# Spreading the running maxima of an mLSTM over the partitions: transpositions into PSUM in place of GpSimd's partition broadcast

## The chip, the cores and the metric

One core of one Trainium2 chip runs the whole program. The metric is the device time of one execution in microseconds, the median of three runs. Times inside an execution come from one profiled execution and are counted from the start of its span.

## The reference, cut to what matters

The program is one layer of an encoder for 512 tokens of 1024 columns, all in float32. Three token mixers work side by side on one input projection: multi-scale pooling, a bidirectional mLSTM with 4 heads of 64, and attention with 8 query heads. Their outputs are concatenated and projected. Then come cross attention into 256 memory tokens and a routed mixture of 16 experts, whose weights (24 MB for each expert) are read from HBM once.

The change touches the mLSTM alone. For one head and one direction, with the running sums b of the forget gates' logarithms and the input gates' logarithms i, it computes (chunks of tokens, `m_st` the running maximum):

```
dmat = where(lower, bcum[j] - bcum[s] + li[s], -inf)
m_j  = maximum(bcum[j] + m_st, max_s dmat[j, s])
a    = exp(dmat - m_j) * (q_j . k_s)
h_j  = sum_s a[j, s] v_s / maximum(|sum_s a[j, s]|, exp(-m_j))
```

With a_s = i_s - b_s and M_j the running maximum of a_s over s up to j (at least 0), the weight of s for j is exp(a_s - M_j), and m_j = b_j + M_j. The backward direction is the same from the last token on.

## The kernel before

Tokens lie on the partitions in four tiles of 128 (`NT`), or along the free dimension, 512 columns, where a row is wanted. Products that need precision are made of a high and a low part, three matmuls in `mm3` (L124 to L127); `split` (L129) makes the parts, a cast on ScalarE (L132) and a subtraction on VectorE or GpSimd (L133).

SBUF is divided into arenas whose words the program hands out and takes back by hand (`Arena`, `Buf`, `Ring`). PSUM has four pools: `mm` with three banks, `tr` and `sc` with two each, and `oo` with one. Tiles of a pool are handed out in the order of the program, so whoever asks for `oo` waits until its last owner has been read.

Two streams of work are emitted in turn by `weave`: a chain and a filler, cut into pieces with an assumed TensorE time. A planner then orders the instructions of each engine by its own estimate of time; every engine works off its list strictly in order. The queue of SP issues all transfers, also in order.

The stages around the change, in order:

- Attention in two halves (L449 to L466): scores, maximum, exponential, scaling by the reciprocal sum (L424 on GpSimd for odd token tiles, L426 on VectorE for even ones), transposition of the weights (L434), product with the values into `oo` (L444). The second half is woven with the mLSTM's projections, in the midst of which `gates()` runs.
- `gates()` (L527): from the gates, per token and for 8 columns (4 heads of each direction), the sums b (`bc`), a (`ag`) and, by a transposition of `az` (L560) and a scan along the free dimension (L562, L564), the running maxima as rows: `Mrow[d]` holds in partition 32 h the row of head h. Four transpositions for each direction (L568) bring them back to tokens on partitions, and L569 adds `bc` to them to make m; L571 makes exp(-m).
- The mLSTM (`mlstm()`, L642) as chain, woven with `fill_kv()` (L731) as filler: the pooling projection, the pooling mixer (`pool_mix()`, L709; sums on GpSimd L714 to L718, VectorE L720 to L722, TensorE L725 into `oo`), and keys and values of the memory. For each head and direction `decay(h, d)` (L621) makes the weights exp(a_s - M_j): the row of M is spread over all partitions, four exponentials on ScalarE (L628) take it with a as bias, and GpSimd masks the diagonal block (`affine_select`, L631). `decay` is called one head ahead. Then come the scores of the head (L650, by `mm3`, into `sc`), their product with the weights on VectorE (L655), the product with the values (L667, into `tr`), the division (L674 to L684) and the norm of the head (L688 to L692). `out_turn` (L635) transposes two heads' outputs through `oo` (L638).
- The output projection: `w_out` is loaded in eight pieces through a ring of three staging buffers (L788), cast and split; `x` is loaded (L807) into words that the mLSTM's buffers had; `out_proj` (L815) adds the product to `x` (L825).
- Cross attention, the choice of tokens, and the experts. Expert weights come in pieces of 1 MB into slots; a slot is opened when the words under it are free, and each load is issued from SP's queue (`issue`, L858; L866, L874).

Of the kernel before, what the change touches and what calls it, by code (L numbers as in the profile page):

```python
# [12 lines left out]
AF = mybir.ActivationFunctionType  # L13
# [16 lines left out]
class Arena:  # L30
    """A stretch of SBUF, one tile, whose words are handed out and taken back by hand."""
# [26 lines left out]
class Buf:  # L58
    """f: its words as float32, r: as float32r. Of several arenas, it lies in the first with room."""
# [39 lines left out]
def build(nc, tc, A, out, ne=NE, dbg=None):  # L99
# [29 lines left out]
    def split(src, h, l, scale=None, le=None):  # L129
        """h + l = src * scale, h of 12 bits."""  # L130
        if scale is None:
            C.copy(h.bitcast(F32R), src)  # L132
            (le or V).tensor_tensor(l.bitcast(F32R), src, h, op=ALU.subtract)  # L133
        else:
            C.activation(h.bitcast(F32R), src, AF.Identity, scale=scale)
            V.scalar_tensor_tensor(l.bitcast(F32R), src, scale, h, op0=ALU.mult, op1=ALU.subtract)
# [19 lines left out]
    # Two streams of work are emitted in turn: generators yield the time on TensorE of each piece.  # L156
# [14 lines left out]
    # ------------------------------------------------------------ constants, small inputs  # L171
# [42 lines left out]
    def load_w(i, parts=2):  # L214
        """Chunk i of the weights, as high and low parts."""
        if i >= len(plan):
            return
        name, src, c0, n = plan[i]
        hb, lb = wring.next(), wring.next()
        st = KT // parts  # L220
        for j in range(parts):
            a, b = j * st, (j + 1) * st
            rbuf = raw.next()
            SP.dma_start(rbuf.f[:, 0:st, :n], src[:, a:b, c0:c0 + n])
            split(rbuf.f[:, 0:st, :n], hb.f[:, a:b, :n], lb.f[:, a:b, :n], le=(G if j % 2 and i < 7 else V))
        W[name] = (hb, lb, n)
# [6 lines left out]
    # ------------------------------------------------------------ x transposed, with the gain, split  # L233
    SP.dma_start(cols.f, A["cols"])
    # the tables of ScalarE and the full clock of TensorE, ahead of the data
# [29 lines left out]
    # ------------------------------------------------------------ tables of the rotation  # L265
# [35 lines left out]
    # ------------------------------------------------------------ products with the chunks  # L301
# [23 lines left out]
    def head_norms(q1, nh):  # L325
        """1 / rms of the nh heads, by token tile."""
# [9 lines left out]
    def rope(t, q1, nh, which, y, variants):  # L336
        """Head norm and rotation of nh heads of a token tile, as [hi, lo] of each."""
# [15 lines left out]
    def turn(t, dest):  # L353
        """[hi; lo] of the heads of a token tile, transposed."""
        p = TR()
        for h in range(4):
            T.transpose(p[:, h * 128:(h + 1) * 128], qsb.f[:, t, h * 128:(h + 1) * 128], idn)
        for h, d in enumerate(dest):
            (C.copy if h % 2 else V.tensor_copy)(d.r[:, t * 128:(t + 1) * 128], p[:, h * 128:(h + 1) * 128])

    # keys and values, then the queries of heads 0 to 3
# [34 lines left out]
    # row of rstd over tokens, on all partitions  # L396
# [9 lines left out]
    # ------------------------------------------------------------ attention  # L406
# [61 lines left out]
    # ------------------------------------------------------------ mLSTM projections, conv  # L468
# [55 lines left out]
    # ------------------------------------------------------------ gates of the mLSTM  # L524
    gs = Mrow = None

    def gates():  # L527
# [3 lines left out]
        nf, ef, lf, bc, ag, mt, em, of = (gs.f[:, i] for i in range(8))  # L531
        V.tensor_scalar(nf, fpre, -1.0, None, op0=ALU.mult)
# [4 lines left out]
        # running sums of log f over tokens, both ways  # L537
# [27 lines left out]
        for d in range(2):  # L565
            p = OO()
            for t in range(NT):
                T.transpose(p[:, t * 128:(t + 1) * 128], Mrow[d].f[:, t * 128:(t + 1) * 128], idn)  # L568
            V.tensor_tensor(mt[:, :, 4 * d:4 * d + 4], p.rearrange("p (t h z) -> p t h z", t=4, z=32)[:, :, :, 0],  # L569
                            bc[:, :, 4 * d:4 * d + 4], op=ALU.add)  # L570
        C.activation(em, mt, AF.Exp, scale=-1.0)  # L571
        az.free()
# [30 lines left out]
    # ------------------------------------------------------------ mLSTM  # L603
    ag, em = gs.f[:, 4], gs.f[:, 6]
    Mb = Ring(f0, 2, [S])
# [5 lines left out]
    # segments of the weights of a direction: tile st covers tokens js  # L611
# [9 lines left out]
    def decay(h, d):  # L621
        """exp(a_s - M_j), s on partitions."""
        c = 4 * d + h
        mb, w = Mb.next(), Wr.next()
        G.partition_broadcast(mb.f, Mrow[d].f[32 * h:32 * h + 1, :])
        for st in range(NT):
            o, js = seg[d][st]
            C.activation(w.f[:, o:o + js.stop - js.start], mb.f[:, js], AF.Exp, scale=-1.0, bias=ag[:, st, c:c + 1])  # L628
# [13 lines left out]
    def mlstm():  # L642
        nxt = [decay(0, 0), decay(0, 1)]
        for h in range(4):
# [40 lines left out]
            # norm of the head, output gate  # L685
# [9 lines left out]
    # ------------------------------------------------------------ pooling mixer, memory keys and values  # L695
# [81 lines left out]
    # ------------------------------------------------------------ output projection  # L777
# [6 lines left out]
    def load_pair(src, k, c0, hb, lb, le=None, scale=None):  # L784
        """Rows of k and k + 1, 512 columns."""
# [14 lines left out]
    for b in (raw, Mb, Wr, hsum, htmp, mst, nst, gs, gt, og, *mv, rows, rrow, ones, tri, *Mrow):  # L800
        b.free()
# [31 lines left out]
    # ------------------------------------------------------------ cross attention  # L833
# [5 lines left out]
    where = {}  # the slot of each chunk under way  # L839
    once = {}  # the slots that serve once, as their words have another use later  # L840
# [3 lines left out]
    # columns of the down projection of the last expert, in parts that end ever sooner  # L844
    LAST = (512, 256, 256)

    def down_part(e, j):
        """The blocks of rows and the columns in chunk j."""
# [9 lines left out]
    def issue(s):  # L858
# [8 lines left out]
        else:  # L867
# [3 lines left out]
            # in halves where TensorE waits for the first one  # L871
# [19 lines left out]
    # router weights, with the gain of the norm  # L891
# [44 lines left out]
    def warm(ap, n):  # L936
        """Keeps TensorE at its full clock while it has to wait; the product is not used."""
# [3 lines left out]
    def top_k(i, j):  # L941
        """The 64 largest of candidates i, in order, to the front of candidates j."""
# [120 lines left out]
    # squares go to words that are written again before they are read  # L1063
# [62 lines left out]
    # ------------------------------------------------------------ ring of expert weights  # L1126
# [13 lines left out]
    # ------------------------------------------------------------ choice of tokens  # L1140
    # the 64 largest of two lists in falling order: the larger of each and its counterpart of the other, reversed
# [3 lines left out]
    # above the threshold, then equal to it, each in the order of the tokens  # L1145
# [20 lines left out]
    def gather(gi, step=4):  # L1166
        """Tokens of two experts, transposed, normed."""
# [29 lines left out]
    # the sum over the experts, in the slots that serve once; x stays as it is until the last gather is done  # L1197
    acc = [s.f.rearrange("p (t d) -> p t d", d=D) for s in once["acc"]]

    def scatter(e, ts, c0, w):  # L1200
        """The columns c0 to c0 + w of the tiles ts, side by side in one bank."""
# [34 lines left out]
    for e in range(ne):  # L1236
# [33 lines left out]
        if e == ne - 1:  # L1270
            # the table of the square root, ahead of its use
# [16 lines left out]
    # ------------------------------------------------------------ the last expert's end, and the final norm  # L1288
# [3 lines left out]
    # the gain of the final norm, along the columns in all partitions  # L1292
# [53 lines left out]
def layout(inp):  # L1346
    """Host side: the small inputs packed, and constants of the shapes."""
# [57 lines left out]
```

## Time and profile before

| what | value |
|---|---|
| median of three runs | 1378.24 us (1375.71, 1378.44, 1378.24) |
| span of the profiled execution, first to last instruction | 1375.2 us; no time of its own is listed beside the three |
| TensorE busy | 1234.7 us, 90% of the span |
| VectorE, ScalarE, GpSimd busy | 443.2, 274.1 and 123.4 us |
| mean granted TensorE clock | 0.965 of full speed |
| read from HBM | 431.74 MB, 315 GB/s over the span |
| chain that ended last | TensorE 61%, DMA 23%, VectorE 7%, issue 4%, ScalarE 3%, GpSimd 1% |

Busy time says how long an engine had an instruction in work; matmuls are pipelined, so their lengths overlap. A full granted clock of 1.00 is 2.4 GHz, 0.50 is 1.2 GHz. Idle time in square brackets stands before an instruction on its own engine, with the instruction that released it; "issue" is time in which the engine waited for nothing that the profile shows. In the rows PE is TensorE, PEld its weight load, DVE VectorE, ACT ScalarE, POOL GpSimd and SP the engine whose queue issues the transfers.

### The profile page before, as it was taken

Reading aid. Unit: us, or ns where it says so; the run is one execution under the profiler, and the core shown is the slowest. Engines: PE = TensorE matmul, PEld = TensorE weight load, DVE = VectorE, ACT = ScalarE, POOL = GpSimd, SP = SyncE. Lnnn points to the kernel's source line nnn. Section 1 sums busy time; section 2 is a strip of 40 time slices with the busy share of each in tenths; the row PEclk is TensorE's granted clock in tenths of the full one; section 3 lists DMA queues with packets and bytes.
Section 4 is the critical chain, followed back from the end, with each engine's and each line's share of the span. In section 5 each row is a group of like instructions: output and inputs, shape, how many; then the busy total and the mean of one; then the engine's idle time right before and its main releaser. Section 6 shows DMA issues by size and latency. Waiting matters only on the chain.

```text
span 1375.2 us, 15752 instructions
## 1 busy us (share of the span) xinstructions
PE 1234.7 (90%) x6225; PEld 632.4 (46%) x6225; DVE 443.2 (32%) x1034; ACT 274.1 (20%) x579; POOL 123.4 (9%) x165
## 2 busy tenths in 40 slices
PE   9999763779998999999999999989988998998886
PEld 8976553668885334334343324323322432332223
DVE  5997731653564011221221221202112120202213
ACT  6565531322441100101001010000101000010113
POOL 5433122220200000000000000000000000000002
PEclk9999975879999999999999999999999999999998
DMA  8321120032587999999999999999999999999996
GB/s 278 90 65 47 52 91 0 31 107 62 213 337 274 367 417 416 419 416 419 414 421 414 420 415 417 418 415 421 414 420 415 417 418 414 420 414 421 415 412 213
DMA packets 97338, 434.87 MB, mean 316 GB/s; under 512 B 7536, under 2 KB 25584, under 8 KB 64496
## 3 DMA queue, kind: packets, MB, share of 16 engines
q1 hardware_dynamic: 97264, 433.87, 78.9%
q8 instruction: 49, 0.80, 0.2%
q14 instruction: 25, 0.20, 0.0%
HBM read 431.74 MB, written 2.10 MB: 315 GB/s over the span
## 4 chain that ended last, share of the span: by engine, by line
PE 61%; DMA 23%; DVE 7%; issue 4%; ACT 3%; POOL 1%; SPq 0%; DVEq 0%; ACTq 0%; POOLq 0%
PE mm L1249 19%; PE sc L1280 8%; PE oo L1249 6%; PE tr L1178 5%; DMA r_f<-in_expert_w_down 4%; PE mm L125 3%; PE mm L127 3%; PE mm L126 3%; DMA rq_f<-in_expert_w_down 3%; DMA ra_f<-in_expert_w_down 3%; DMA rb_f<-in_expert_w_gu 3%; DMA rq_f<-in_expert_w_gu 3%; DMA r2a_f<-in_expert_w_gu 3%; PE tr L1206 2%; PE tr L1207 2%
## 5 line engine op out<-in xcount | busy, mean ns | idle before, releaser
L1216 DVE SCALAR_TENSOR_TENSOR f_f<-tr,f_f 128x512 f32<-128x512 f32 x112 | 79.9, 746 | 91.5 <-PE tr L1207 91.5
L1249 PE MATMUL mm<-rq_f,rg_f 128*64 128x512 f32 x388 | 97.3, 604 | 6.6 <-DMA rq_f<-in_expert_w_gu 6.6
L133 DVE TENSOR_TENSOR rp_r<-sc,rp_r 128x512 fp32r<-128x512 f32 (+1 forms) x31 | 21.1, 682 | 216.1 <-ACT rp_r L132 216.1
L1249 PE MATMUL mm<-r_f,rg_f 128*64 128x512 f32 x324 | 80.3, 602 | 5.8 <-DMA r_f<-in_expert_w_gu 5.4
L1299 POOL TENSOR_SCALAR f_f<-f_f 128x128 f32<-128x128 f32 x8 | 3.3, 433 | 907.5 <-PE tr L1194 880.4
L1178 PEld LDWEIGHTS tr<-f_f 128*128 128x128 f32 x512 | 61.7, 191 | 45.6 <-issue 23.5
L1178 PE MATMUL tr<-f_f 128*128 128x128 f32 x512 | 70.8, 284 | 7.5 <-ACT rg_f L1185 4.7
L1262 DVE TENSOR_TENSOR fb_f<-mm,fb_f 128x512 f32<-128x512 f32 x16 | 11.1, 692 | 204.9 <-PE mm L1249 199.0
L1261 ACT ACTIVATE fb_f<-mm 128x512 f32<-128x512 f32 x32 | 19.0, 597 | 278.6 <-PE mm L1249 278.6
L1280 PE MATMUL sc<-rq_f,fb_f 128*64 128x512 f32 x280 | 64.7, 599 | 3.7 <-DMA rq_f<-in_expert_w_down 3.6
L1185 ACT ACTIVATE rg_f<-tr,f_f 128x128 f32<-128x128 f32 x32 | 11.8, 368 | 271.7 <-PE tr L1178 181.6
L1249 PE MATMUL mm<-rb_f,rg_f 128*64 128x512 f32 x240 | 59.6, 603 | 3.8 <-DMA rb_f<-in_expert_w_gu 3.8
L1183 DVE TENSOR_SCALAR rg_f<-tr,f_f 128x128 f32<-128x128 f32 x32 | 11.2, 351 | 157.7 <-PE oo L1249 78.7
L1280 PE MATMUL sc<-r_f,fb_f 128*64 128x512 f32 x240 | 57.3, 600 | 4.5 <-DMA r_f<-in_expert_w_down 4.5
L1206 PE MATMUL tr<-rp_r 128*128 128x512 f32 (+1 forms) x132 | 58.1, 444 | 3.3 <-ACT rp_r L132 1.4
L132 ACT CAST rp_r<-sc 128x512 fp32r<-128x512 f32 (+1 forms) x31 | 17.9, 579 | 200.1 <-PE sc L1280 200.1
L1207 PE MATMUL tr<-rp_r 128*128 128x512 f32 (+1 forms) x132 | 53.2, 407 | 1.8 <-DVE rp_r L133 1.1
L1206 PEld LDWEIGHTS tr<-rp_r 128*128 128x128 f32 x132 | 24.5, 187 | 55.8 <-DVE f_f L1216 31.5
L1249 PEld LDWEIGHTS mm<-rq_f,rg_f 128*64 128x64 f32 x388 | 24.3, 136 | 55.5 <-issue 34.6
L1249 PE MATMUL mm<-r2a_f,rg_f 128*64 128x512 f32 x192 | 46.5, 603 | 3.4 <-DMA r2a_f<-in_expert_w_gu 3.4
L127 PE MATMUL mm<-r_r,rb_r 128*128 128x256 f32 (+2 forms) x160 | 46.7, 296 | 0.0
L1249 PE MATMUL oo<-rq_f,rg_f 128*64 128x512 f32 x172 | 45.1, 593 | 0.0
(452 smaller groups left out, 2225.0 us busy)
## 6 DMA issues: line engine op xcount, KB each, us to landing
rq_f<-in_expert_w_gu SPq DMA_DIRECT2D x70, 1024.0 KB, 19.8
r_f<-in_expert_w_gu SPq DMA_DIRECT2D x54, 1024.0 KB, 19.8
rb_f<-in_expert_w_gu SPq DMA_DIRECT2D x45, 1024.0 KB, 19.8
rq_f<-in_expert_w_down SPq DMA_DIRECT2D x35, 1024.0 KB, 20.0
r2a_f<-in_expert_w_gu SPq DMA_DIRECT2D x32, 1024.0 KB, 19.8
r_f<-in_expert_w_down SPq DMA_DIRECT2D x30, 1024.0 KB, 20.0
ra_f<-in_expert_w_gu SPq DMA_DIRECT2D x26, 1024.0 KB, 19.9
rb_f<-in_expert_w_down SPq DMA_DIRECT2D x18, 1024.0 KB, 18.9
```

The costliest lines, as they stand in the source:

```text
L125: T.matmul(o, lh, rh, start=start, stop=False)
L126: T.matmul(o, lh, rl, start=False, stop=False)
L127: T.matmul(o, ll, rh, start=False, stop=stop)
L132: C.copy(h.bitcast(F32R), src)
L133: (le or V).tensor_tensor(l.bitcast(F32R), src, h, op=ALU.subtract)
L1178: i = T.matmul(o, x.f[:, t, kt * 128:(kt + 1) * 128], flat(g.f[:, t]), start=(t == 0), stop=(t == NT - 1))
L1206: T.matmul(pp[:, i * w:(i + 1) * w], GT.r[:, ts_], flat(yh.r)[:, cs], start=True, stop=False)
L1207: T.matmul(pp[:, i * w:(i + 1) * w], GT.r[:, ts_], flat(yl.r)[:, cs], start=False, stop=True)
L1216: V.scalar_tensor_tensor(ao, p, g, ao, op0=ALU.mult, op1=ALU.add)
L1249: T.matmul(pg[2 * half + b][64 * ab:64 * ab + 64], xs.f[:, k, el * 64:(el + 1) * 64], wv[:, :, ab], start=(k == 0), stop=(k == KT - 1))
L1261: C.activation(hsl.f[:, b], pg[b], AF.Silu)
L1280: T.matmul(py[c][64 * ab:64 * ab + 64], hT.f[:, blk, 64 * ab:64 * ab + 64], wv[:, ab, c * 512:(c + 1) * 512], start=(blk == 0), stop=(blk ...
```

## The change

`gates()` keeps the running maxima by token, before the addition of `bc`, in `mk_`, the words of `nf`, whose content is no longer needed there. `decay()` spreads a column of it: for each token tile the column is read as a 128x128 block (the same column 128 times) and transposed into a quarter of an `oo` bank, so that every partition holds the row M_j. ScalarE's exponentials read that bank. The ring `Mb` of two rows in SBUF is gone, and the rows `Mrow` are given back at the end of `gates()`.

```diff
@@ gates()
         nf, ef, lf, bc, ag, mt, em, of = (gs.f[:, i] for i in range(8))
+        mk_ = nf
 ...
             p = OO()
             for t in range(NT):
                 T.transpose(p[:, t * 128:(t + 1) * 128], Mrow[d].f[:, t * 128:(t + 1) * 128], idn)
-            V.tensor_tensor(mt[:, :, 4 * d:4 * d + 4], p.rearrange("p (t h z) -> p t h z", t=4, z=32)[:, :, :, 0],
-                            bc[:, :, 4 * d:4 * d + 4], op=ALU.add)
+            V.tensor_copy(mk_[:, :, 4 * d:4 * d + 4], p.rearrange("p (t h z) -> p t h z", t=4, z=32)[:, :, :, 0])
+        V.tensor_tensor(mt, mk_, bc, op=ALU.add)
         C.activation(em, mt, AF.Exp, scale=-1.0)
-        az.free()
+        for b in (az, *Mrow):
+            b.free()
@@ ahead of the mLSTM
-    Mb = Ring(f0, 2, [S])
@@ decay(h, d)
         c = 4 * d + h
-        mb, w = Mb.next(), Wr.next()
-        G.partition_broadcast(mb.f, Mrow[d].f[32 * h:32 * h + 1, :])
+        mb, w = OO(), Wr.next()
+        for t in range(NT):
+            T.transpose(mb[:, t * 128:(t + 1) * 128], gs.f[:, 0, t, c:c + 1].to_broadcast([128, 128]), idn)
         for st in range(NT):
             o, js = seg[d][st]
-            C.activation(w.f[:, o:o + js.stop - js.start], mb.f[:, js], AF.Exp, scale=-1.0, bias=ag[:, st, c:c + 1])
+            C.activation(w.f[:, o:o + js.stop - js.start], mb[:, js], AF.Exp, scale=-1.0, bias=ag[:, st, c:c + 1])
@@ after the mLSTM
-    for b in (raw, Mb, Wr, hsum, htmp, mst, nst, gs, gt, og, *mv, rows, rrow, ones, tri, *Mrow):
+    for b in (raw, Wr, hsum, htmp, mst, nst, gs, gt, og, *mv, rows, rrow, ones, tri):
```

With `Mb` and `Mrow` gone, buffers that are handed out later lie elsewhere. In the arena `f0`, `Wr` moves from word 3208 to 2696 and the norm statistics `nst` from 1544 to 1032; `x` later takes words 376 to 4472, 1024 for each token tile. In `rq`, the pooling input `up` moves from word 7020, the words of `az`, to 5988, where `Mrow` (5996 to 7020) was. Comments are left out of the changed file as well.

## Rows read from the trace of the kernel before

**Rows 1.** The profile's page, its parts 1 and 2: busy time, share of the span and instructions of each engine; then the span in 40 equal slices of 34.4 us, in tenths.

```profile
PE 1234.7 (90%) x6225; PEld 632.4 (46%) x6225; DVE 443.2 (32%) x1034; ACT 274.1 (20%) x579; POOL 123.4 (9%) x165
...
PE   9999763779998999999999999989988998998886
...
PEclk9999975879999999999999999999999999999998
DMA  8321120032587999999999999999999999999996
```

**Rows 2.** Busy time by stretches: the stretch (us), its length, then for each engine the busy us and in brackets the number of instructions, the granted TensorE clock as a share of full speed, the DMA share and GB/s. First pieces of the stretch, then the whole stretch and its neighbours.

```profile
174.20:180.30 6.10, 6.06 (x29) 6.06 (x30) 2.04 (x7) 2.91 (x4) 2.09 (x2) 0.50 0.06 16
207.30:211.10 3.80, 3.75 (x11) 3.18 (x12) 0.38 (x1) 3.80 (x10) 0.79 (x1) 0.51 0.00 0
232.50:239.10 6.60, 6.60 (x24) 5.63 (x24) 1.17 (x2) 0.00 (x0) 0.71 (x2) 0.50 0.00 0
248.70:251.90 3.20, 3.19 (x9) 2.16 (x10) 3.03 (x12) 0.69 (x1) 0.60 (x3) 0.50 0.48 159
251.90:273.50 21.60, 21.60 (x150) 19.60 (x149) 17.18 (x56) 7.94 (x15) 5.75 (x14) 1.00 0.07 26
282.70:296.10 13.40, 13.40 (x52) 12.31 (x53) 9.59 (x32) 2.50 (x3) 2.36 (x1) 0.50 0.12 40
...
165.90:309.50 143.60, 87.79 (x476) 75.41 (x474) 57.15 (x160) 37.87 (x67) 34.47 (x52) 0.74 0.18 61
100.00:165.90 65.90, 62.30 (x328) 42.88 (x326) 53.40 (x111) 38.56 (x88) 17.80 (x20) 1.00 0.13 39
309.50:420.00 110.50, 105.18 (x652) 92.68 (x652) 62.57 (x192) 42.84 (x104) 13.66 (x19) 1.00 0.56 216
```

**Rows 3.** TensorE in order of time, the first instruction after each hole: start, length, line, operation, output and input, shape; in square brackets the idle time before it and what released it.

```profile
174.24 1.12 PE L434 MATMUL tr<-f_f,fb_f 128*128 128x128 f32 x4 [8.07 <-POOL fb_f L424]
207.35 0.79 PE L125 MATMUL sc<-rc_r,r2a_r 128*128 128x512 f32 x1 [10.26 <-DVE f_f L655]
232.47 1.12 PE L667 MATMUL tr<-rq_f,f_f 128*128 128x65 f32 x4 [18.36 <-DVE f_f L655]
248.71 2.08 PE L725 MATMUL oo<-rq_f 128*128 128x512 f32 x2 [9.47 <-DVE rq_f L722]
282.70 0.77 PE L125 MATMUL sc<-rc_r,r2a_r 128*128 128x512 f32 x1 [9.12 <-DVE f_f L675]
```

**Rows 4.** GpSimd in order of time, the same columns.

```profile
173.51 0.68 POOL L424 TENSOR_SCALAR fb_f<-fb_f,f_f 128x512 f32<-128x512 f32 x1 [6.83 <-issue]
199.37 0.28 POOL L631 TENSOR_SCALAR_AFFINE_SELECT f_f<-f_f 128x128 f32<-128x128 f32 x1
205.79 0.80 POOL L625 PARTITION_BROADCAST f_f<-rq_f  x1 [6.14 <-issue]
206.67 0.55 POOL L631 TENSOR_SCALAR_AFFINE_SELECT f_f<-f_f 128x128 f32<-128x128 f32 x2
207.33 0.79 POOL L625 PARTITION_BROADCAST f_f<-rq_f  x1
246.23 1.25 POOL L718 TENSOR_TENSOR fb_f<-rq_f 64x512 f32<-64x512 f32 x1 [6.85 <-issue]
273.42 2.33 POOL L133 TENSOR_TENSOR rg_r<-rq_f,rp_r 128x1024 fp32r<-128x1024 f32 x1 [8.29 <-PE oo L638]
```

**Rows 5.** The line of the broadcast: kinds of instruction with their number, shortest, median and longest duration in ns, first and last start.

```profile
L625 POOLq MODIFY_POOL_CONFIG  x12: 1/8/15, 160.2 to 249.5; - x12
L625 POOL PARTITION_BROADCAST f_f<-rq_f x8: 794/804/1153, 165.9 to 257.8; - x8
```

**Rows 6.** The chain of waits that ended last, from 155 to 310 us: shares by line, then pieces with start and length.

```profile
by line: issue 24.9%; PE tr L667 12.5%; PE mm L125 5.6%; PE mm L126 5.1%; PE mm L127 4.9%; DMA rq_f<-in_ca_wkv 3.5%; DMA f_f<-in_x 3.3%; PE sc L125 2.7%; PE oo L444 2.3%; DMA rq_f<-in_w_out 2.2%; ACT f_f L628 2.2%; PE sc L127 2.0%; PE sc L1
272.44 0.45 PE oo L638 x4
275.78 3.46 DMA rq_f<-in_w_out
```

**Rows 7.** Groups of instructions by line, engine, operation and shape, 100 to 310 us for ScalarE: number, busy us, mean ns of one, idle us before them with its releasers. Then, in the same columns, all exponentials of the decay (100 to 420 us, their four shapes together) and the attention's transpositions; then two lines by themselves, with shortest, median and longest duration in ns.

```profile
L421 ACT ACTIVATE fb_f<-sc,f_f 128x512 f32<-128x512 f32 x22 | 15.3, 693 | 8.6 <-DVE f_f L419 7.3 <-DVE f_f L422 1.3
L628 ACT ACTIVATE f_f<-f_f 128x512 f32<-128x512 f32 x8 | 5.6, 710 | 13.8 <-POOL f_f L625 13.8
...
L628 ACT ACTIVATE f_f<-f_f 128x384 f32<-128x384 f32 (+3 forms) x32 | 15.3, 550 | 48.0 <-POOL f_f L625 48.0
...
L434 PE MATMUL tr<-f_f,fb_f 128*128 128x128 f32 x96 | 14.8, 282 | 8.1 <-POOL fb_f L424 8.1
...
L638 PE MATMUL oo<-f_f,rq_f x8: 270/272/273, 272.3 to 305.9; 128*128 128x128 f32 x8
...
L569 DVE TENSOR_TENSOR f_f<-oo,f_f x2: 174/174/175, 176.2 to 182.1; 128x16 f32<-128x16 f32 x2
```

**Rows 8.** What SP's queue of transfers waited for (us in total, times, longest us), then rows of SP's and DVE's order of time.

```profile
SPq L866 <- PE mm L127: 30.4, 3, 14.8
...
297.24 4.75 SPq L807 DMA_DIRECT2D f_f<-in_x  x4
327.21 0.34 SPq L866 DMA_DIRECT2D rc_f<-in_expert_w_gu  x1
...
308.74 0.68 DVE L825 TENSOR_TENSOR f_f<-mm,f_f 128x512 f32<-128x512 f32 x1
```
## The prediction

> **What bounds the kernel now.** I read the busy rows and the slices first [rows 1]. TensorE is busy nine tenths of the span and the DMA share stands at its top from the middle on, so the expert stage is limited by the weight stream and TensorE together. Only one place has slack: the TensorE digits read 7, 6, 3, 7, 7 in the slices from 138 to 309 us, and the granted clock falls to 5 with them. Nobody is at its limit there; somebody waits.
>
> Second, busy time by stretches [rows 2]. From 165.9 to 309.5 us, 143.6 us long, TensorE is busy 87.8 us at a mean clock of 0.74, while the neighbouring stretches run 95% busy at 1.00. Third, TensorE's order of time has five holes in it, 8.1 + 10.3 + 18.4 + 9.5 + 9.1 = 55.3 us [rows 3]. Each is followed by a piece in which TensorE is fully busy at clock 0.50, which is 1.2 GHz: 6.1 + 3.8 + 6.6 + 3.2 + 13.4 = 33.1 us [rows 2], half of which, 16.5 us, is lost to the clock. Those who end the holes are GpSimd's `L424` scaling, DVE `L655` twice (a product with the decay weights), DVE `L722` (pooling) and DVE `L675`. Fourth, GpSimd's own order of time [rows 4]: before each switch between `partition_broadcast` (`L625`) and an ordinary elementwise instruction it stands still 6.1 to 6.9 us and waits for nothing that the profile shows ("issue"). Two broadcasts in a row cost nothing extra (the row at 207.33: no idle), and `affine_select` follows at once on either kind (206.67, 199.37). `MODIFY_POOL_CONFIG` stands on the line of the broadcast, 12 times [rows 5], as many as there are such switches: a swap of GpSimd's code, twelve times some 6 us. What is behind GpSimd in its strict order waits along: attention's last scaling, the masks on the weights, the pooling sums.
>
> Four holes follow directly. `L424` waits for a swap (first hole). The masks that release `L655` sit behind a broadcast, which sits behind a swap (second and third). The pooling's `L718`, 6.85 us late, releases `L722` (fourth). The fifth is a reading: GpSimd's `L133` begins 8.29 us after its last mask, the row names a TensorE instruction as releaser [rows 4], but it is the first elementwise instruction after the last broadcast. It frees a staging buffer; the `w_out` transfer lands 3.46 us after that [rows 6], and the cast and the subtraction that wait for it stand in DVE's queue ahead of `L675`. As a check, the chain of waits from 155 to 310 us puts 24.9%, 38.6 us, on "issue" [rows 6].
>
> **The change part by part.** *Removed*: eight broadcasts, 6.8 us busy on GpSimd [rows 5], and every switch, as no other broadcast is in the kernel. Gone with them, if nothing takes their place, are the five holes and the half-speed pieces: 143.6 - 55.3 - 16.5 = 71.8 us of TensorE work at full clock.
>
> *Added on TensorE*: 8 x 4 transpositions of 128x128 into the one `oo` bank. Nothing now broadcasts a column this way in this stretch, but four fp32 transpositions into `oo` stand on the chain with 0.45 us (`L638`) [rows 6]: 8 x 0.45 = 3.6 us. From below: 0, hidden in gaps. From above: each alone at its row length of 0.272 us [rows 7], 32 x 0.272 = 8.7 us. I take 3.6, as four in a row is exactly the form added. The sum is then 75.4 us of TensorE work.
>
> The Trainium skill, "TensorE: Matmul & The Clock Gate", Part 4, gives about 275 ns for a PE-mode transpose in a kernel and says that transposes don't raise the clock as matmuls do; by its figure the term would be 8.8 us, an estimate, and the time 5 us longer. What the rule does to the clock is a rival below.
>
> *Unavoidable idle time*: the neighbours on both sides, which have the same kind of woven work, are 62.3/65.9 and 105.2/110.5 busy [rows 2], so 95%: 75.4/0.95 = 79.4 us. DVE is busy 57.2 us in the old stretch, 72% of 79.4; in the neighbour before it is 81% busy with TensorE still at 95%, so DVE does not become the bound.
>
> *A new wait*: `decay` draws the `oo` bank in program order. It queues behind attention's last output tile (split off by ScalarE and DVE), then each decay waits for the four exponentials of the one before: 4 x 0.550 = 2.2 us [rows 7], and the transpositions wait at the head of TensorE's queue with everything behind them: the filler products and the next scores. One turn is 2.2 + 0.45 = 2.65 us, eight are 21.2 us. Below: 0, as seven of eight are asked for a head ahead and the planner puts other products between. I take 5 us, about two turns: the first head's pair, which nothing precedes. The exponentials then read PSUM in place of SBUF; attention's, which read 512 columns from PSUM, take 0.693 us against 0.710 from SBUF [rows 7], so nothing is charged.
>
> *Small edits, together nothing*: two copies and one addition replace two additions of 0.174 us [rows 7] in the gates; with 26 us of DVE slack in the stretch they cost at most 0.5 us. The maxima now wait for the gates' transpositions rather than for the scan alone; TensorE has the memory-key products to do meanwhile, and without that cover it is about 1 us. *Moved memory*: the pooling input now lies on the words of the freed maxima, so its two PSUM banks are held until the gates' transpositions have read those; I put that at 0 to 3 us and inside the 5. The norm statistics now lie under the first row tile of `x` instead of the second, so its load, issued at 297.24 [rows 8], waits for the last norm, 3.5 us at most; the addition that needs it comes at 308.74, after the landing either way.
>
> *Sum*: the stretch becomes 79.4 + 5 = 84.4 us instead of 143.6; 59.2 us go. I take 58, one microsecond off for the small edits and the moved memory. *Does it reach the end?* Behind 309.5 us TensorE is 95% busy, and the expert weights are requested only as words come free: SP's queue waits 30.4 us in three goes for products that must free the words of its first expert loads, of which the earliest goes out at 327.21 [rows 8]. So the stream starts earlier with the work and nothing is given back. The profiled span is 1375.2 us, 3.0 below the median of 1378.2; from the median, 1378.2 - 58 = **1320 us**.
>
> **The rivals.** *B, the bank becomes the wait*: all eight turns exposed, 16 us over my 5, so 1336, and up to 1353 if short stops hold the clock at 0.50 for as long as now (16.5 us). For it: one bank, TensorE in strict order, and the pooling, the output turns and attention on the same bank. Against: weights are asked for one head ahead, and 251.9 to 273.5, where the weights were there, is 21.6 us solid [rows 2]. The fifth hole staying (9.1 + 6.7 us) gives about the same time, 1336. *C, the swaps stay in part*: if `affine_select` against elementwise also needs one in an order not seen, say six of twelve stay: half the gain, 1349. Against: the rows show it after both kinds without idle time. *D, the stretch shrinks but the weight stream does not move*: 1378. Against: the waits of SP's queue above.
>
> *E, slower*: the clock. TensorE's stretch becomes many short bursts with transpositions and stops, and the clock stays at 1.2 GHz throughout: 75.4 x 2 = 151 us, plus 21.2 us of turns, 172 us instead of 143.6: 1407 us. It decides against the change from the point where the stretch exceeds 143.6 us, that is, if over three fifths of the 75.4 us run at half clock with all the stops exposed: 75.4 x 1.62 + 21.2. For it: the 13.4 us at 0.50 after 282.7, although TensorE was solidly busy [rows 2]. Against: the attention's transpositions (96 of them, with 0.28 us each) run in the neighbour at clock 1.00 [rows 2, 7]. The Trainium skill's rule named above, that transposes don't count as busy, would speak for E; the trace disagrees as far as they are mixed with products.
>
> **How the numbers follow.** Forecast 0.72, B 0.14, C 0.05, D 0.04, E 0.05. The forecast's own bounds: no extra idle time gives 143.6 - 71.8 = 72 us at best, 1306; 8.7 us of transpositions and 10 us of stalls leave a stretch of 94.7 us, 1329. To hold 8 in 10 the range reaches through B's first price and to C: 1306 to 1350. A change under 0.2% (2.8 us) can't be told from none here. Faster: forecast, B and C, 0.91; within 0.2%: D, 0.04; slower: E, 0.05.
>
> **What would show it.** Right: no `MODIFY_POOL_CONFIG`, no 6 us "issue" on GpSimd, TensorE at 95% and clock near 1.00 from 166 to about 250 us, the transpositions at about 0.45 us per four, the first expert load some 58 us before 327 us, the expert stage of unchanged length. Wrong: TensorE idle before the decay's transpositions with ScalarE as releaser (B), swaps left (C), expert loads that start where they do now (D), clock 0.50 over the stretch (E).

## The result and the profile after

| kernel | median, us | runs, us | span of the profiled execution, us |
|---|---|---|---|
| before | 1377.58 | 4, 1375.71 to 1378.44 | 1375.2 |
| after | 1321.91 | 4, 1321.58 to 1325.01 | 1320.2 (its time 1321.95) |

The ratio is 0.9591, 95% interval 0.9579 to 0.9603. The spans differ by 55.0 us. One execution of experiment 12, slow with 1403.98 us at a granted clock of 0.845 where its others have 0.99, is left out of its number below.

The page of the kernel after, its parts 1 and 2, against [rows 1]: TensorE has no dip left, its clock digits are 9 up to the last slice, and the rise of the DMA digits comes earlier.

```profile
PE 1227.5 (93%) x6257; PEld 625.9 (47%) x6257; DVE 448.4 (34%) x1035; ACT 273.7 (21%) x579; POOL 115.8 (9%) x157
...
PE   9899898999989999999999899889989998998885
...
PEclk9999999999999999999999999999999999999998
DMA  8221040317879999999999999999999999999995
```

Busy time by stretches of the kernel after, columns as in [rows 2]. The second row is the changed stretch: it starts at the same time as before's and ends with the first TensorE instruction behind the addition of `x` (309.48 before, 254.58 after, 54.9 us earlier). It is 88.7 us long instead of 143.6. The first and third rows are the neighbours, and they are as before. Of the 55.0 us, then, 54.9 are won in this stretch and none is given back later.

```profile
100.00:165.90 65.90, 62.30 (x323) 42.59 (x322) 53.38 (x110) 39.80 (x90) 18.31 (x18) 1.00 0.12 38
165.90:254.60 88.70, 80.37 (x522) 69.69 (x520) 63.02 (x165) 37.59 (x68) 28.72 (x45) 0.96 0.31 104
254.60:365.10 110.50, 105.13 (x652) 92.64 (x652) 62.10 (x191) 43.03 (x104) 13.64 (x19) 0.99 0.56 215
204.00:222.00 18.00, 14.87 (x95) 12.40 (x93) 17.06 (x41) 6.95 (x14) 6.74 (x10) 1.00 0.17 59
228.50:234.00 5.50, 5.46 (x24) 4.89 (x25) 3.50 (x15) 2.08 (x6) 1.55 (x6) 0.59 0.00 0
234.00:244.00 10.00, 10.00 (x57) 9.02 (x57) 9.10 (x25) 2.99 (x4) 2.35 (x1) 0.89 0.16 52
```

TensorE in order of time, kernel after, all stops of more than 0.6 us in that stretch. Where [rows 3] had five of 8 to 18 us, these seven are 8.3 us together.

```profile
174.58 3.65 PE L444 MATMUL oo<-f_f,rq_f 128*64 128x512 f32 x16 [0.65 <-DVE f_f L570]
183.72 0.65 PE L627 MATMUL oo<-f_f 128*128 128x128 f32 x4 [1.02 <-DVE rd_r L133]
216.89 0.66 PE L669 MATMUL tr<-rq_f,f_f 128*128 128x65 f32 x4 [2.43 <-DVE f_f L657]
220.75 1.12 PE L727 MATMUL oo<-rq_f 128*128 128x512 f32 x2 [0.70 <-DVE ra_r L136]
228.54 0.65 PE L627 MATMUL oo<-f_f 128*128 128x128 f32 x4 [1.93 <-ACT f_f L630]
251.11 0.50 PE L126 MATMUL mm<-r_r,rb_r 128*128 128x512 f32 x1 [0.85 <-POOL r_r L133]
254.58 0.50 PE L125 MATMUL mm<-r_r,rb_r 128*128 128x512 f32 x1 [0.70 <-DVE f_f L827]
```

GpSimd in order of time, kernel after. Masks (`L633`) follow elementwise work, and the other way round, with no swap between them, and no `MODIFY_POOL_CONFIG` stands on any of its lines. What the 4.80 us of "issue" at 178.03 wait for the profile doesn't show; nobody on the chain waits for this row.

```profile
170.22 0.11 POOL L700 MEMSET rq_f<- 128x16 f32 x1 [4.49 <-PE oo L569]
...
170.46 1.62 POOL L716 TENSOR_TENSOR rq_f<-rq_f 128x527 f32<-128x527 f32 x1
...
178.03 1.07 POOL L716 TENSOR_TENSOR rq_f<-rq_f 128x527 f32<-128x527 f32 x1 [4.80 <-issue]
...
202.94 3.24 POOL L133 TENSOR_TENSOR rg_r<-rq_f,rp_r 128x1024 fp32r<-128x1024 f32 x1 [1.55 <-PE mm L127]
...
208.03 0.94 POOL L633 TENSOR_SCALAR_AFFINE_SELECT f_f<-f_f 128x128 f32<-128x128 f32 x3 [0.17 <-ACT f_f L630]
209.60 2.35 POOL L133 TENSOR_TENSOR r_r<-rq_f,r_r 128x1024 fp32r<-128x1024 f32 x1 [0.63 <-ACT r_r L132]
```

The line of the new transpositions: number, shortest, median and longest duration in ns. Each takes 273 ns, as the transpositions of [rows 7].

```profile
L627 PE MATMUL oo<-f_f x32: 270/273/323, 183.7 to 228.9; 128*128 128x128 f32 x32
```

The chain of waits from 155 to 255 us, shares by line: "issue" is 4.3% of 100 us, against 24.9% of 155 us in [rows 6].

```profile
by line: PE tr L669 8.9%; DMA rq_f<-in_w_out 7.7%; DMA rq_f<-in_ca_wkv 6.8%; DVE f_f L657 5.3%; DVE r_r L133 4.8%; issue 4.3%; PE mm L125 3.3%; DVE rq_f L686 3.3%; PE oo L627 3.1%; PE mm L126 3.0%; DVE f_f L143 2.9%; DVE f_f L141 2.8%; PE m
```

SP's order of time: the first expert load goes out at 272.31, where [rows 8] had 327.21, again 54.9 us earlier; the wait of that line for products is as long as it was.

```profile
272.31 0.34 SPq L868 DMA_DIRECT2D rc_f<-in_expert_w_gu  x1
...
SPq L868 <- PE mm L127: 31.1, 3, 15.5
```

### The profile page after: what moved, and what is told of

The parts are those of the page before. It is cut to its first block, busy times and chain, and to the rows that moved or that the text cites. A ratio compares the mean times of both kernels' runs of the same rounds, so it can differ in the third digit from the quotient of the medians.

```text
span 1320.2 us, 15788 instructions
## 1 busy us (share of the span) xinstructions
PE 1227.5 (93%) x6257; PEld 625.9 (47%) x6257; DVE 448.4 (34%) x1035; ACT 273.7 (21%) x579; POOL 115.8 (9%) x157
## 3 DMA queue, kind: packets, MB, share of 16 engines
q1 hardware_dynamic: 97264, 433.87, 82.2%
## 4 chain that ended last, share of the span: by engine, by line
PE 60%; DMA 25%; DVE 8%; ACT 3%; issue 1%; SPq 0%; POOL 0%; DVEq 0%; ACTq 0%; POOLq 0%
PE mm L1251 19%; PE sc L1282 9%; PE oo L1251 6%; PE tr L1180 5%; DMA r_f<-in_expert_w_down 5%; DMA rq_f<-in_expert_w_gu 5%; DMA rq_f<-in_expert_w_down 3%; DMA ra_f<-in_expert_w_down 3%; DMA rb_f<-in_expert_w_gu 3%; DMA r2a_f<-in_expert_w_gu 3%; PE mm L125 3%; PE mm L127 3%; PE mm L126 3%; PE tr L1208 2%; PE tr L1209 2%; DMA r_f<-in_expert_w_gu 2%
## 5 line engine op out<-in xcount | busy, mean ns | idle before, releaser
L1251 PEld LDWEIGHTS mm<-rq_f,rg_f 128*64 128x64 f32 x388 | 24.3, 136 | 55.7 <-issue 34.6
```

The source lines that it names most:

```text
L1251: T.matmul(pg[2 * half + b][64 * ab:64 * ab + 64], xs.f[:, k, el * 64:(el + 1) * 64], wv[:, :, ab], start=(k == 0), stop=(k == KT - 1))
```

## The experiments

Theory A: the swaps of GpSimd's code cost the time, and any version without them is as fast. Rivals: the broadcast itself or the length of its way is what cost (then the transpositions are the gain), and in the kernel after the `oo` bank, the transpositions or the moved memory hold something back. Ratios are to the kernel before, run beside each group (its medians there: 1378.48, 1377.91 and 1378.57), with 95% intervals.

| experiment | median, us | ratio |
|---|---|---|
| the change | 1321.91 | 0.9591 [0.9579, 0.9603] |
| 1 broadcasts back, unused | 1334.76 | 0.9689 [0.9673, 0.9706] |
| 2 kernel before without swaps | 1316.60 | 0.9555 [0.9541, 0.9570] |
| 3 `w_out` off GpSimd, in before | 1366.83 | 0.9923 [0.9908, 0.9939] |
| 4 `mm` banks for the rows | 1320.16 | 0.9579 [0.9564, 0.9593] |
| 5 sixteen swaps, in after | 1405.79 | 1.0206 [1.0189, 1.0222] |
| 6 after with the edit of 2 | 1315.82 | 0.9550 [0.9535, 0.9564] |
| 7 four times the transpositions | 1327.53 | 0.9639 [0.9626, 0.9652] |
| 8 old memory layout | 1316.49 | 0.9564 [0.9548, 0.9579] |
| 9 `Mrow` kept, `Mb` not | 1317.68 | 0.9563 [0.9545, 0.9581] |
| 10 8 and 3 | 1315.90 | 0.9545 [0.9525, 0.9565] |
| 11 8 and 6 | 1316.88 | 0.9556 [0.9537, 0.9574] |
| 12 8, 3 and 4 | 1320.37 | 0.9581 [0.9563, 0.9600] |

**1. The broadcasts back, for nobody.** In the kernel after, on before's memory layout (experiment 8), `decay` also broadcasts the row into SBUF, and a copy of one column reads it.

```diff
+        G.partition_broadcast(m2.f, Mrow[d].f[32 * h:32 * h + 1, :])
 ...
+        C.copy(sm.f[:, 62:63], m2.f[:, 0:1])
```

> The changed kernel with the eight broadcasts put back beside the transpositions, on the memory layout of before; the decay weights still come from PSUM, and what a broadcast delivers is read by nothing but a one-column copy on ScalarE. Theory (the swaps of GpSimd's code hold its queue and whoever stands in it): the 12 swaps of some 6.5 us come back, and with them the holes: 1360 to 1385 us. Rival (what was late was the broadcast's result, on which the exponentials waited): the weights no longer need it, so eight broadcasts of 0.85 us and eight copies of 0.2 us are hidden or nearly so: 1322 to 1330 us.

Both numbers were missed: 12.8 us over the change, and 18.3 us over experiment 8, which has the same memory layout. The planner put the eight broadcasts into two groups, and only four swaps are left. GpSimd in order of time, then TensorE's two holes of 5 us and more:

```profile
166.25 0.80 POOL L626 PARTITION_BROADCAST f_f<-rq_f  x1 [5.68 <-DVE rq_f L711]
...
175.22 0.69 POOL L424 TENSOR_SCALAR fb_f<-fb_f,f_f 128x512 f32<-128x512 f32 x1 [7.05 <-issue]
...
186.67 1.14 POOL L626 PARTITION_BROADCAST f_f<-rq_f  x1 [8.58 <-PE oo L444]
...
199.76 1.05 POOL L718 TENSOR_TENSOR rq_f<-rq_f 128x527 f32<-128x527 f32 x1 [6.78 <-issue]
```

```profile
175.96 1.12 PE L434 MATMUL tr<-f_f,fb_f 128*128 128x128 f32 x4 [8.57 <-POOL fb_f L424]
204.11 1.12 PE L671 MATMUL tr<-rq_f,f_f 128*128 128x65 f32 x4 [5.04 <-DVE f_f L659]
```

The first hole of [rows 3] is back although no exponential needs the broadcast. It is the queue behind the swap that waits.

**2. The kernel before, broadcasts kept, swaps gone.** What is ordinary elementwise work on GpSimd in this stretch goes to VectorE: the last attention head's scaling, the pooling sums, the subtractions of `w_out`.

```diff
-        if t % 2:
+        if t % 2 and h < 7:
 ...
-            G.tensor_tensor(sA.f[:, 1:PW], u[:, 0:PW - 1], u[:, 1:PW], op=ALU.add)
+            V.tensor_tensor(sA.f[:, 1:PW], u[:, 0:PW - 1], u[:, 1:PW], op=ALU.add)
 ...
-            load_pair(w_out, k, c * 512, wo_h[c, k].f, wo_l[c, k].f, le=(G if i % 2 else V))
+            load_pair(w_out, k, c * 512, wo_h[c, k].f, wo_l[c, k].f, le=V)
```

> The kernel before, with its broadcasts, but with the ordinary elementwise work that GpSimd had between them moved to VectorE: the last odd attention scalings, the seven sums of the pooling mixer and the four subtractions of the w_out pieces. Theory (swaps): with nothing to swap for, at most one or two swaps stay; VectorE has some 10 us more to do (4 x 1.23, 7 x 0.66 and 2 x 0.48 us), partly exposed: 1322 to 1340 us. Rival (the broadcast itself, or SBUF against PSUM, is the price): 1370 to 1388 us.

1316.60 us: faster than the change, without one transposition more, and below the range of the theory too, which had expected 1322 to 1340 us. (The sums moved are six, not seven.) GpSimd in order of time: one swap in, and then broadcasts and masks take turns without stops of that kind.

```profile
168.18 0.80 POOL L625 PARTITION_BROADCAST f_f<-rq_f  x1 [5.33 <-DVE rq_f L564]
...
186.81 0.80 POOL L625 PARTITION_BROADCAST f_f<-rq_f  x1
187.68 0.75 POOL L631 TENSOR_SCALAR_AFFINE_SELECT f_f<-f_f 128x128 f32<-128x128 f32 x2
188.52 0.80 POOL L625 PARTITION_BROADCAST f_f<-rq_f  x1
```

There is a second swap, for the next elementwise instruction. Its rows stand at 219.3 us, and the instruction comes at 294.51, with no 6 us behind the VectorE instruction that releases it: a swap costs nothing where no work waits behind it.

```profile
L1002 POOLq MODIFY_POOL_CONFIG  x2: 11/11/11, 219.3 to 219.4; - x2
```

```profile
294.51 0.96 POOL L1002 TENSOR_SCALAR f_f<-f_f 128x256 f32<-128x256 f32 x2 [75.19 <-DVE f_f L143]
```

The rival that the transpositions are the gain falls: the broadcast alone, with its 0.8 us, costs nothing measurable.

**3. The fifth hole.** Of the edit above only the last line, in the kernel before.

> The kernel before, with only the four w_out subtractions moved from GpSimd to VectorE. This is for the fifth hole. If GpSimd's first w_out subtraction was late because of a swap, one swap goes: 9.1 us of idle time and 6.7 us of half clock go, some of it comes back as 4 x 1.23 us on VectorE: 1360 to 1372 us. If it waited for TensorE, as the row names it, the time stays: 1375 to 1381 us.

1366.83 us. TensorE in order of time: four holes as in [rows 3], of which the first is shown, and in the fifth one's place 1.40 us.

```profile
174.83 1.11 PE L434 MATMUL tr<-f_f,fb_f 128*128 128x128 f32 x4 [8.62 <-POOL fb_f L424]
...
274.74 0.47 PE L125 MATMUL sc<-rc_r,r2a_r 128*128 128x512 f32 x1 [1.40 <-DVE f_f L655]
```

The fifth hole was a swap, in spite of the TensorE instruction that the row names as releaser, and it was worth 11.65 us. The swap itself is still made: its rows now stand at 269.7 us on `L1002`, which starts at 348.64, so nothing waits for it.

**4. The other PSUM pool.**

```diff
-        mb, w = OO(), Wr.next()
+        mb, w = MM(), Wr.next()
```

> The changed kernel with the transpositions of the maxima into the mm pool (three banks) instead of oo (one). Forecast's term: the turns on the one bank are exposed with about 5 us, of which 0 to 5 go, but the filler has fewer mm banks: 1317 to 1326 us. Rival B (the one bank is the wait, 21 us of turns): 1305 to 1312 us.

1320.16 us, which the intervals don't tell from the change. Rival B as priced here did not come. But the time doesn't price the turns on the one bank, since the move also changes what is done ahead of the stretch. Busy time by stretches in this kernel, columns as above, the second row up to the same mark:

```profile
100.00:165.90 65.90, 55.55 (x285) 34.86 (x285) 51.84 (x114) 40.70 (x93) 18.64 (x21) 0.97 0.16 52
165.90:252.40 86.50, 85.07 (x561) 75.42 (x557) 62.97 (x161) 36.67 (x66) 27.53 (x42) 1.00 0.26 88
```

In the stretch TensorE's idle time falls from 8.3 to 1.4 us and its clock is 1.00 instead of 0.96; the stops in front of the transpositions are gone. Ahead of it TensorE is busy 55.6 us instead of 62.3, with a stop of 4.10 us at 122.91, and does the missing work within the stretch (561 matmuls recorded there instead of 522). The two nearly cancel; what the turns alone cost stays open.

**5. Sixteen swaps.** In the kernel after, on before's memory layout, behind the masks of each `decay`: a broadcast of a row of its weights into an unused buffer and one ordinary addition there.

```diff
+        m2 = Mb.bufs[0].f
+        G.partition_broadcast(m2, w.f[0:1, 0:S])
+        G.tensor_tensor(m2[:, 0:4], m2[:, 0:4], m2[:, 4:8], op=ALU.add)
```

> The changed kernel on the memory layout of before, where after the masks of each decay GpSimd broadcasts one finished row of the weights into a spare buffer and then adds four columns of it: eight broadcasts, each followed by an elementwise instruction, 16 swaps in the stretch, and nobody needs the outcome (the products that write the weights in place wait for the broadcast to have read them). Theory (swaps in GpSimd's queue set the stretch): GpSimd has 28.7 us of its own work there, 16 x 6.5 us of swaps and 8 x 0.8 us of broadcasts, 139 us, so the stretch is again about 140 us: 1365 to 1390 us. Rival (the gain came from the path of the data or from the freed memory): 1322 to 1335 us.

1405.79 us, above what was expected, and slower than before. GpSimd in order of time, then the line of the broadcast, who waited for it, and the line of the addition:

```profile
196.46 0.80 POOL L636 PARTITION_BROADCAST f_f<-f_f  x1 [5.65 <-issue]
...
204.42 0.19 POOL L637 TENSOR_TENSOR f_f<-f_f 128x4 f32<-128x4 f32 x1 [6.90 <-issue]
```

```profile
L636 POOLq MODIFY_POOL_CONFIG  x16: 1/1/11, 190.8 to 304.9; - x16
L636 POOL PARTITION_BROADCAST f_f<-f_f x8: 802/802/802, 196.5 to 310.7; - x8
...
  DVE f_f L660: 79.1, 8
```

```profile
L637 POOLq MODIFY_POOL_CONFIG  x16: 118/123/129, 197.4 to 311.8; - x16
```

The expectation priced the swaps alone; here the broadcast also reads the weights, so DVE's `L660` waits until it has read them, 79.1 us in eight goes, and TensorE behind it. So not all of the loss is the swaps' hold on GpSimd's own queue. Each switch has its stop, in both directions, around instructions that nobody needs.

**6. The change with the edit of 2.** No ordinary elementwise work on GpSimd in the stretch and no broadcast either.

> The changed kernel with the same moves to VectorE as in the second experiment (last odd attention scalings, pooling sums, w_out subtractions), so that transpositions and broadcasts stand against each other with no swap on either side. Forecast's terms: 3.6 us of transpositions and up to 5 us of turns make it 2 to 9 us slower than the 1316.6 of the broadcasts: 1319 to 1325 us. Rival (transpositions and turns are hidden): 1313 to 1318 us.

1315.82 us, equal to experiment 2 and within the rival's range: the 2 to 9 us for transpositions and turns did not show. Without swaps, broadcasting and transposing cost the same.

**7. Three more sets of transpositions**, each into the same quarter of the bank.

```diff
-        for t in range(NT):
+        for t in [t for _ in range(4) for t in range(NT)]:
```

> The changed kernel with each of the 32 transpositions done four times over. Forecast's term (3.6 us on TensorE's path, which is 95% busy): 3 x 3.6 = 10.8 us more, 1330 to 1335 us. Rival (they lie in gaps of TensorE): at most 3 us more, 1321 to 1325 us.

1327.53 us, 5.6 over the change, between both expectations: 1.9 us for a set of 32. The stretch up to the same mark:

```profile
165.90:260.30 94.40, 88.71 (x615) 78.77 (x613) 61.48 (x164) 37.80 (x68) 28.15 (x45) 0.98 0.29 97
```

Busy time times clock gives the work at full clock, as an estimate: 88.71 x 0.98 - 80.37 x 0.96 = 9.8 us more, 3.3 for a set, close to the 3.6 of the forecast. The time grew by less because TensorE also has 2.6 us less idle time and a higher clock; why, the runs don't show.

**8. The old memory layout.** `Mb` and `Mrow` are kept, unused, until the mLSTM's end, so that all later buffers lie as before the change.

```diff
-        for b in (az, *Mrow):
-            b.free()
+        az.free()
@@
+    Mb = Ring(f0, 2, [S])
```

> The changed kernel with the memory layout of before: Mb stays allocated and unused, Mrow is given back where it was. Forecast's term for the moved memory (0 to 3 us, the pooling input on the words of the maxima): 1318 to 1322 us. Rival (the freed memory gives a part of the gain): over 1324 us.

1316.49 us, 5.4 less than the change by the medians and 3.7 by the ratios, whose intervals touch; 0 to 3 had been put. GpSimd's and DVE's order of time in this kernel:

```profile
161.94 0.11 POOL L700 MEMSET rq_f<- 128x16 f32 x1 [0.21 <-PE oo L561]
...
165.91 1.06 POOL L716 TENSOR_TENSOR rq_f<-rq_f 128x527 f32<-128x527 f32 x1
...
183.77 1.57 POOL L716 TENSOR_TENSOR rq_f<-rq_f 128x527 f32<-128x527 f32 x1 [14.46 <-DVE rq_f L724]
```

```profile
166.79 0.67 DVE L709 TENSOR_TENSOR rq_f<-mm,f_f 128x512 f32<-128x512 f32 x1
```

and DVE's in the kernel after:

```profile
174.45 0.68 DVE L709 TENSOR_TENSOR rq_f<-mm,f_f 128x512 f32<-128x512 f32 x1
```

The pooling input (`L709`) lies on `Mrow`'s words in the kernel after. Its first memset waits for the gates' transpositions (`PE oo L569`, above) until 170.22 instead of 161.94, and its second half comes 7.7 us later. The first block's sums start 4.6 us later for it (`L716`, 170.46 above), but the second block's start 5.7 us earlier (178.03 against 183.77). By which wait the moved input reaches the time is therefore not shown. Of the four stops of the kernel after at 174.58, 183.72, 216.89 and 220.75, 4.8 us together, TensorE shows here only one of 0.63 us. Its stretch ends at 251.34, 3.2 us before the change's. This profiled execution, of 1319.69 us, is the slowest of its four, which may be why it shows less than the 5.4 us of the medians.

**9. Only `Mrow` kept.** The first hunk of 8 without `Mb`, to part the pooling input from `x` and the norm statistics, which still lie as in the change.

> The changed kernel with Mrow given back only after the mLSTM, Mb still gone: the pooling input lies where it was before, the norm statistics and the decay weights stay where the change has them. The old layout as a whole was 5.4 us faster than the change. Theory (the pooling input on the words of the maxima waits for the gates and holds two mm banks): all of it, 1315 to 1318 us. Rival (the load of x waits for the norm statistics under its first tile): none of it, 1320 to 1323 us.

1317.68 us, ratio 0.9563 against 0.9564 in 8: what lies on `Mrow`'s words is nearly all of it, the pooling input and the work buffers that come to lie elsewhere with it (`L717` writes to the arena `rq` in the change, to `fb` in 8 and 9). That `x` lies under the norm statistics costs nothing that could be measured.

**10 to 12. Together.** The old layout with the edit of 3, with that of 6, and with those of 3 and 4.

> The changed kernel on the memory layout of before, with the w_out subtractions on VectorE. In the change three small VectorE instructions last 2.3 us instead of 0.2 to 0.4 while GpSimd makes such a subtraction. If that costs the path: some 2 x 3 = 6 us less, 4 x 1.23 us more on VectorE, and a shorter way for the staging buffers: 1311 to 1315 us. If VectorE's own load decides: 1316 to 1319 us.

> The same, with the pooling sums and the last odd attention scalings on VectorE too, which in the change's own layout gave 6 us. If the gains of layout and moves add up: 1310 to 1313 us. If both take away the same wait (the late start of the pooling): 1314 to 1317 us.

> The old layout with w_out on VectorE and the transpositions into the mm pool. The turns on the one oo bank, the last of which leaves TensorE idle for 1.9 us and then at half clock, go: 2 to 4 us less than without the move of the bank: 1308 to 1313 us. If the filler lacks the mm banks: no gain or up to 3 us more.

1315.90, 1316.88 and 1320.37 us: 10 lies between its two ranges, 11 in that of the same wait, and 12 above both of its own. The gains don't add up: with the old layout, the moves or both, the kernel comes to rest near 1316 us. With the `mm` banks it is 4.5 us slower, and ahead of the stretch TensorE is again busy only 55.9 us, as in 4. What sets the 1316 stays open. The best versions beat the change by 4 to 6 us and cannot be told apart among themselves.

**What a swap costs.** The stretch from 165.9 us to the end marked above, all with before's memory layout, each from its profiled execution. The third column counts the swaps that fall into the stretch with work behind them: the first swap of 1, 3 and before is over when the stretch starts, give or take 0.4 us, and nothing waits for the last one of 3. The last column is the length above that without swaps, by swap of the third column.

| kernel | swaps | in the stretch, with work behind | stretch, us | us for each |
|---|---|---|---|---|
| 8 | 0 | 0 | 85.4 | |
| 1 | 4 | 3 | 98.7 | 4.4 |
| 3 | 12 | 10 | 137.0 | 5.2 |
| before | 12 | 11 | 143.6 | 5.3 |
| 5 | 16 | 16 | 171.9 | 5.4 |

The execution of 8 is 3.2 us above the median of its kernel. If that lies in the stretch, the base is 82.2 us by estimate (9 has 83.1), and the four prices are 5.5, 5.5, 5.6 and 5.6 us. So a swap with work behind it costs some 4.4 to 5.6 us of the path, and that the price rises with their number is not shown.

## Why the prediction was right, point by point

**The cause** was right, and it is shown, not only argued: taking the swaps away without the change gives the whole gain (2), putting four or sixteen back takes part or all of it away again (1, 5; in 5 a wait for the broadcast's reading adds to it). The Trainium skill, "GPSIMD Engine Reference", section 2.1, says that the first call to a freshly loaded routine pays a load of some 6 us without a visible instruction. The rows agree in size (5.65 us in experiment 5 before a broadcast), and they show it at every switch, 6.90 us on the way back too.

**Readings to set right.** Of the twelve stops before a swap in the kernel before, nine read "issue", 5.9 to 7.1 us, not 6.1 to 6.9; the other three name an instruction as releaser, with 5.6, 9.8 and 8.3 us. The third hole holds two swaps, not one: GpSimd stands still 5.91 us before the broadcast at 223.09 and 6.75 us before `L717` at 230.64, and the masks that TensorE waits for come behind both.

**One step of the reasoning was a coincidence.** I took the 12 rows of `MODIFY_POOL_CONFIG` on the broadcast's line [rows 5] for the twelve switches. Experiment 5 has 16 on the broadcast's line for its eight switches to a broadcast: a swap leaves two rows on the line that needs it. In the kernel before, six of the twelve swaps stand on `L625`, and the others on the elementwise lines, the fifth hole's among them:

```profile
L133 POOLq MODIFY_POOL_CONFIG  x2: 8/8/8, 265.2 to 265.2; - x2
```

That row would have shown the fifth hole to be a swap, before any experiment.

**The holes and the clock**: the five holes and the pieces at clock 0.50 went, apart from what follows the stop at 228.54: 5.5 us at a mean of 0.59 and 10 us at 0.89.

**The sum**: 59.2 us were worked out and 58 taken; the spans differ by 55.0 and the medians by 55.7. The terms:

- *TensorE's work, clock and idle time.* 84.4 us were forecast for the stretch, of them 75.4 work at full clock, 4 idle and 5 turns. It is 88.7 us: 80.4 busy and 8.3 idle, so TensorE is 91% busy and not 95%. Of the busy time the two pieces behind 228.5 us lose 5.46 x 0.41 + 10.0 x 0.11 = 3.3 us to the clock, which the forecast had at full speed and without a price; the work itself is near 77.0 us. The clock is thus the larger part of the 4.3 us by which the stretch is longer than forecast.
- *Transpositions.* 3.6 us forecast; some 3.3 for a set of 32 by experiment 7, of which 1.9 reached the time. One takes 273 ns by its row, but in a row they overlap, four of them 0.65 us at 183.72. By the Trainium skill's 275 ns each ("TensorE: Matmul & The Clock Gate", Part 4) the term was 8.8 us, an estimate; the length of one agrees with the row, the sum does not.
- *Turns of the `oo` bank.* 5 us forecast. The stops in front of `L627` are 1.02 and 1.93 us, two as forecast, the first behind attention's last output tile, the second behind the exponentials. As stops they are 3 us; the half clock that follows the second was not in the term. Experiment 4 does not price them alone.
- *Moved memory.* This is the term that was mis-sized: 0 to 3 us, put "inside the 5". Of the two parts I named the right one, the pooling input on the maxima's words, but priced only the two banks held. It cost some 4 to 5 us (8, 9), and by which wait is open. Without it TensorE idles 4.9 us (8: 80.5 busy of 85.4), against the 9 put for idle time and turns together. So idle time and turns were put some 4 us too high, the moved memory some 4 and the clock 3.3 us too low. They cancel in part: that the gain came within 2.3 us of the 58 owes something to luck.
- *VectorE "does not become the bound"* was true of the time and wrong in one place: from 204 to 222 us it is busy 17.06 of 18 us and TensorE waits for it. Yet adding its share of GpSimd's work there lost nothing (6, 11).

**The shift to the end**: nothing was given back, as the waits of SP's queue had let one expect; D is out. B is out by TensorE's rows, with two stops of 1.02 and 1.93 us in front of the transpositions where it had eight turns; C by the rows of GpSimd; and E by the clock of 0.96 in a stretch with 32 transpositions in it. The one line that speaks for a part of E, the half clock after a stop, is worth 3.3 us.

## What to carry to other kernels

When GpSimd stands still for some 6 us with "issue" in front of an instruction, look whether the last different kind of work was a routine such as the broadcast and whether `MODIFY_POOL_CONFIG` stands on the line, and count the switches, not the instructions: it is enough to keep one of the two kinds off the engine for a stretch, whichever is easier to move. The cost appears elsewhere, as holes on the engine whose buffers the waiting queue should have released, and then as a lower clock. When a buffer is freed early, look at who gets its words next and what that one now waits for; here this took back up to a tenth of the gain.

## What the runs showed of the hardware that I had not expected

- A swap is paid in both directions, and the mask (`affine_select`) and the memset follow either kind without one. Each costs some 5 us of the path where work waits behind it (the table above), and nothing where GpSimd has no work due (2, 3).
- When a small VectorE instruction starts beside a GpSimd subtraction of 128x1024, it lasts until that ends (three cases in the kernel after, 2.25 to 2.60 us). VectorE in order of time, kernel after, beside GpSimd's rows at 202.94 and 209.60 above: the same line takes 0.15 us once and 2.25 us the next time.

```profile
208.66 0.15 DVE L141 SCALAR_TENSOR_TENSOR f_f<-f_f 128x4 f32<-128x4 f32 x1
...
209.72 2.25 DVE L141 SCALAR_TENSOR_TENSOR f_f<-f_f 128x4 f32<-128x4 f32 x1
```

  These stand on the chain, and still taking GpSimd's subtractions away won nothing on the old layout (10, 11).
- A stop of 1.93 us at 228.54 was followed by a clock of 0.59 and one of 2.43 us at 216.89 was not (1.00 from 204 to 222). What decides between them no run here shows.
